# A four-layer decoder trunk in split float32: five buffers for raw weights instead of three

## The chip, the cores and the metric

The kernel runs on one core of a Trainium2 chip. The metric is the device time of one execution in microseconds: the median of three runs of the kernel before is 860.79 us (860.39, 860.79 and 860.89). Beside those runs, one execution was recorded by the hardware profiler; it took 859.14 us, and its span from the first to the last instruction is 857.4 us, so 1.74 us lie outside the span. Trace times below are microseconds from the start of the span.

## The reference

The input x is 256 tokens of 1024 float32 values. Four residual layers follow each other, and a final norm; the third kind of mixer stands between a gated DeltaNet layer and a second pooling layer:

```python
for i in range(DEPTH):                      # 4
    kind, j = i % N_MIXERS, i // N_MIXERS   # 0, 1, 2, 0
    h = rmsnorm(x, norm_g[i])
    if kind == 0:
        y = pool_mixer(h, pool_w_in[j], pool_w_grp[j], pool_scale[j], pool_w_out[j])
    elif kind == 1:
        y = gdn_mixer(h, gdn_w_in[j], gdn_conv[j], gdn_a_log[j], gdn_dt_bias[j],
                      gdn_norm_g[j], gdn_w_out[j])
    else:
        y = mla_mixer(h, positions, ...)
    x = x + y.astype(x.dtype)
return rmsnorm(x, final_g)
```

The gated DeltaNet mixer works on chunks of 64 tokens. The part of it on which the argument below turns is a triangular solve in each of 8 heads:

```python
L = jnp.where(strict, jnp.einsum('bhnid,bhnjd->bhnij', k_beta, k) * decay, 0.0)
A = jnp.eye(C, dtype=L.dtype) + L
sol = lax.linalg.triangular_solve(A, rhs, left_side=True, lower=True)
```

where k comes out of the input projection, a causal convolution over four tokens, SiLU and a normalization over 128 channels.

## The kernel before

Nearly all work is matrix products of the 256 tokens with weights, in float32 by splitting: a matrix is written as a high part that TensorE can take in one pass, and a low part, the rest. Three products (high by high, high by low, low by high) are added in PSUM.

**A unit of weights** is two k-slices of 128 rows by 512 columns, 512 KB (some are single slices or 256 KB). The function `weights` brings it in: SP's queue issues the DMA (L104, or L108 for other layouts) into a tile `raw` of the pool `rawp` (4 KB in each of the 128 partitions); ScalarE casts each slice to the high part `whi` (L117); VectorE, for some slices POOL, subtracts it from `raw` to get `wlo` (L119). `whi` and `wlo` are tiles of the pool `ring`, nine places of 128x512 for each name. A raw place is free again when the subtraction of its second slice is done; a place in the ring when TensorE's last product with it is done. TensorE then does 24 products of 128x256 (L127, L128, L129), or as many columns in pieces of 512 (L167).

**What sets the order.** The kernel is written once, stage after stage. A scheduler orders the instructions of each engine when the kernel is built; it knows how many places each pool has, and so which DMA can be issued when. On the chip each engine then runs its list in order, waiting on semaphores. Pools without a number of places (the residuals and large tiles `s4`, the scratch pools `wa`, `wb`, `wh`, the PSUM pools) are sized by the same build. The first six units of the program are single slices (k0 to k5 of the first projection) in scratch places, not in `rawp`.

**The start.** SP loads x in four DMAs (L256), two for each of the two token tiles, gains (L276) and the first weights. Each tile is normalized (L209 on ScalarE, L291 on POOL, L303 and L308) and transposed by TensorE (L323, eight transposes a tile); then come the products k0 to k7 of the first projection for that tile.

**The DeltaNet layer** projects by parts named g0 to g3 (gates), k0, k1 (keys), q0, q1 (queries) and v0 to v3 (values). After k1: convolution on ScalarE and VectorE (L633, L636), SiLU to `kqT` (L669), transposes on TensorE (L675), squares and sums for the norm (L678, L679), powers on POOL (L657), the scale (L705), the products kT by kT (L688), and the matrix `LT` (L692 on VectorE). Then the triangular solve, in this order:

- SP writes the diagonal blocks (32x32) of `LT` to DRAM, `d_l`, in eight DMAs, four for each token tile (L718), and reads them back in another layout, `Lb` (L721);
- POOL does 31 steps of forward substitution, a product `pr` (L726) and a subtraction into `Tb` (L730) each;
- SP writes `Tb` to DRAM, `d_t` (L732), and reads it back as `T` in eight DMAs (L736);
- TensorE puts the inverses of the blocks together, with copies by VectorE and ScalarE between: per token tile L806 (with T and LT), copy L808, L812, subtraction L815 (the stage "pairs"); then transposes L820, copy to T on ScalarE L821, products L824, copy to X on VectorE L827, products L830, subtraction L833 (the stage "whole").

Beside this TensorE projects what does not need the solve: queries, values and gates. The values' transposes are L778, their scaling on ScalarE is L781, and L847 multiplies them by the inverse. From L869 on the recurrence over chunks runs. The output projection uses the weights `gdn_w_out`.

Of the kernel before, what the change touches and what calls it, by code (L numbers as in the profile page):

```python
# [42 lines left out]
def trunk(ctx: ExitStack, tc: tile.TileContext, x, positions, norm_g, pool_w_in, pool_w_grp,  # L43
# [10 lines left out]
    E1 = 4  # L54
    const = ctx.enter_context(tc.tile_pool(name="const", bufs=1))
    s4 = ctx.enter_context(tc.tile_pool(name="s4"))
    rawp = ctx.enter_context(tc.tile_pool(name="rawp", bufs=3))
    ring = ctx.enter_context(tc.tile_pool(name="ring", bufs=9))
    wa = ctx.enter_context(tc.tile_pool(name="wa"))
    wb = ctx.enter_context(tc.tile_pool(name="wb"))  # L60
# [1169 lines left out]
def build(inputs, **opts):  # L1230
    import numpy as np
    import concourse.bacc as bacc

    nc = bacc.Bacc("TRN2", target_bir_lowering=False, num_devices=1)
    arrays, args = {}, []
    for name in _INS:
        a = np.ascontiguousarray(inputs[name])
        arrays[f"in_{name}_dram"] = a
        args.append(nc.dram_tensor(f"in_{name}_dram", a.shape, mybir.dt.from_np(a.dtype),
                                   kind="ExternalInput").ap())  # L1240
    args.append(nc.dram_tensor("out_0_dram", inputs["x"].shape, F32, kind="ExternalOutput").ap())
    with tile.TileContext(nc, schedule_with_timeline_sim=True, auto_bufs=True) as tc:
        trunk(tc, *args, **opts)
    return nc, arrays
# [8 lines left out]
```

## Time and profile before

| | |
|---|---|
| median of the runs | 860.79 us (860.39 to 860.89) |
| the profiled execution | 859.14 us |
| its span | 857.4 us |
| mean granted TensorE clock | 0.990 |
| read from HBM | 137.79 MB, 163 GB/s over the span |

The profile's page gives the busy time of each engine and groups of instructions (line, engine, operation, tiles written and read, count, busy time, mean time in ns, idle time ahead of it and what ended that). Engine names: PE is TensorE, PEld its weight loads, DVE VectorE, ACT ScalarE, SP the engine whose queue (SPq) issues nearly all DMAs. The trace answers further views: waits (who waited for which line, in total, how often, the longest), windows (busy time and granted TensorE clock in stretches of time), the timeline of one engine, and the chain of waits that ended last. In the windows, TensorE is busy this much of each 100 us:

```profile
0.00:100.00 100.00, 94.05 (x690) 89.46 (x691) 72.29 (x132) 60.38 (x110) 16.11 (x73) 0.98 0.64 202
100.00:200.00 100.00, 99.61 (x702) 91.75 (x701) 62.52 (x110) 56.53 (x105) 13.30 (x19) 1.00 0.59 185
200.00:300.00 100.00, 100.00 (x769) 95.72 (x768) 81.91 (x181) 64.18 (x124) 62.04 (x76) 1.00 0.56 169
300.00:400.00 100.00, 91.61 (x551) 80.22 (x550) 61.78 (x121) 50.71 (x126) 25.58 (x55) 0.95 0.33 100
400.00:500.00 100.00, 99.62 (x711) 93.22 (x710) 65.01 (x120) 59.65 (x128) 13.10 (x28) 1.00 0.61 177
500.00:600.00 100.00, 100.00 (x732) 93.76 (x731) 74.64 (x161) 56.55 (x131) 6.12 (x4) 1.00 0.58 154
600.00:700.00 100.00, 99.62 (x680) 90.29 (x679) 69.79 (x159) 58.48 (x144) 7.58 (x14) 1.00 0.47 143
700.00:800.00 100.00, 100.00 (x812) 98.37 (x811) 73.70 (x109) 58.08 (x98) 4.79 (x10) 1.00 0.61 194
```

The columns are: length; busy time (and instructions) of PE, PEld, DVE, ACT, POOL; granted clock; share of the DMA engines; GB/s. The first and the fourth row are those with idle time: the start, and the stretch around the triangular solve (the DeltaNet layer runs from about 200 to 400 us).

### The profile page before, as it was taken

Reading aid. Unit: us, or ns where it says so; the run is one execution under the profiler, and the core shown is the slowest. Engines: PE = TensorE matmul, PEld = TensorE weight load, DVE = VectorE, ACT = ScalarE, POOL = GpSimd, SP = SyncE. Lnnn points to the kernel's source line nnn. Section 1 sums busy time; section 2 is a strip of 40 time slices with the busy share of each in tenths; the row PEclk is TensorE's granted clock in tenths of the full one; section 3 lists DMA queues with packets and bytes.
Section 4 is the critical chain, followed back from the end, with each engine's and each line's share of the span. In section 5 each row is a group of like instructions: output and inputs, shape, how many; then the busy total and the mean of one; then the engine's idle time right before and its main releaser. Section 6 shows DMA issues by size and latency. Waiting matters only on the chain.

```text
span 857.4 us, 16137 instructions
## 1 busy us (share of the span) xinstructions
PE 835.0 (97%) x5967; PEld 778.7 (91%) x5967; DVE 591.2 (69%) x1138; ACT 488.2 (57%) x1007; POOL 155.7 (18%) x292
## 2 busy tenths in 40 slices
PE   7999999999999969999999999999999999999996
PEld 6999998988999959888979998999989989999986
DVE  4589776456989665656577659778767668866852
ACT  5565555467857435555565654566555476555542
POOL 4000000233248941022212002000000210000012
PEclk9999999999999989999999999999999999999999
DMA  6765556546555462222547676743652547565551
GB/s 199 249 188 188 178 189 213 180 148 206 188 160 176 134 168 102 75 74 99 173 147 215 201 165 172 196 132 95 171 167 79 173 149 218 175 192 183 187 200 50
DMA packets 111288, 140.43 MB, mean 164 GB/s; under 512 B 23340, under 2 KB 53224, under 8 KB 111208
## 3 DMA queue, kind: packets, MB, share of 16 engines
q1 hardware_dynamic: 109056, 138.17, 53.1%
q8 instruction: 47, 0.77, 0.4%
q0 software_dynamic: 320, 1.06, 0.3%
q10 hardware_dynamic: 1832, 0.16, 0.2%
q14 instruction: 33, 0.27, 0.1%
HBM read 137.79 MB, written 1.58 MB: 163 GB/s over the span
## 4 chain that ended last, share of the span: by engine, by line
PE 85%; POOL 7%; DVE 2%; DMA 2%; issue 2%; ACT 1%; SPq 1%; POOLq 0%; ACTq 0%; DVEq 0%
PE acc L167 34%; PE acc L127 12%; PE acc L128 12%; PE acc L129 12%; POOL Tb L730 2%; POOL pr L726 2%; PE aux L127 2%; PE aux L128 2%; PE aux L129 2%; DVE h L303 1%; DMA gain<-in_norm_g_dram 1%; PE aux L688 1%; ACT junk L209 1%; PE aux L806 1%; PE tp L1165 1%
## 5 line engine op out<-in xcount | busy, mean ns | idle before, releaser
L119 DVE TENSOR_TENSOR wlo<-raw,whi 128x512 fp32r<-128x512 f32 (+1 forms) x491 | 338.6, 712 | 163.2 <-ACT whi L117 160.9
L117 ACT CAST whi<-raw 128x512 fp32r<-128x512 f32 (+1 forms) x508 | 301.4, 617 | 261.8 <-PE acc L167 89.8
L127 PE MATMUL acc<-hTh,whi 128*128 128x256 f32 x832 | 235.3, 283 | 1.0 <-DVE cv L636 1.0
L128 PE MATMUL acc<-hTl,whi 128*128 128x256 f32 x832 | 235.8, 283 | 0.0
L129 PE MATMUL acc<-hTh,wlo 128*128 128x256 f32 x832 | 234.7, 282 | 0.0
L127 PEld LDWEIGHTS acc<-hTh,whi 128*128 128x128 f32 x832 | 157.7, 190 | 1.8 <-issue 1.4
L128 PEld LDWEIGHTS acc<-hTl,whi 128*128 128x128 f32 x832 | 157.6, 189 | 0.4
L129 PEld LDWEIGHTS acc<-hTh,wlo 128*128 128x128 f32 x832 | 157.5, 189 | 0.2
L167 PE MATMUL acc<-wlo,yTh 128*128 128x256 f32 (+1 forms) x384 | 116.2, 319 | 0.0
L167 PE MATMUL acc<-whi,yTh 128*128 128x256 f32 (+1 forms) x384 | 116.2, 323 | 0.0
L167 PE MATMUL acc<-whi,yTl 128*128 128x256 f32 (+1 forms) x384 | 92.4, 321 | 0.0
L167 PEld LDWEIGHTS acc<-wlo,yTh 128*128 128x128 f32 x384 | 72.0, 188 | 5.0
L167 PEld LDWEIGHTS acc<-whi,yTh 128*128 128x128 f32 x384 | 71.9, 188 | 5.2
L167 PEld LDWEIGHTS acc<-whi,yTl 128*128 128x128 f32 x384 | 63.1, 188 | 5.6
L291 POOL TENSOR_TENSOR hg<-x,gain 128x256 f32<-128x256 f32 x18 | 14.8, 832 | 259.1 <-DVE x L353 257.4
L167 PE MATMUL acc<-wlo,hTh 128*128 128x512 f32 (+1 forms) x144 | 55.9, 394 | 0.4 <-DVE wlo L119 0.2
L167 PE MATMUL acc<-whi,hTh 128*128 128x512 f32 (+1 forms) x144 | 55.5, 393 | 0.7 <-ACT hTh L195 0.7
L167 PE MATMUL acc<-whi,hTl 128*128 128x512 f32 (+1 forms) x144 | 45.4, 388 | 0.0
L119 POOL TENSOR_TENSOR wlo<-raw,whi 128x512 fp32r<-128x512 f32 x17 | 23.1, 1360 | 70.2 <-ACT whi L117 70.2
L434 POOL COPY win<-u 128x4 f32<-128x4 f32 x8 | 2.8, 354 | 177.0 <-ACT u L428 177.0
L167 PEld LDWEIGHTS acc<-wlo,hTh 128*128 128x128 f32 x144 | 27.3, 190 | 6.8 <-DVE wlo L119 1.7
L167 PEld LDWEIGHTS acc<-whi,hTh 128*128 128x128 f32 x144 | 27.3, 190 | 6.8 <-ACT hTh L195 1.7
(337 smaller groups left out, 1443.3 us busy)
## 6 DMA issues: line engine op xcount, KB each, us to landing
raw<-in_pool_w_in_dram SPq DMA_DIRECT2D x60, 512.0 KB, 4.4
raw<-in_gdn_w_in_dram SPq DMA_DIRECT2D x48, 512.0 KB, 3.9
raw<-in_pool_w_out_dram SPq DMA_DIRECT2D x32, 512.0 KB, 3.7
raw<-in_mla_w_in_dram SPq DMA_DIRECT2D x24, 512.0 KB, 4.4
raw<-in_mla_w_uq_dram SPq DMA_DIRECT2D x36, 256.0 KB, 3.8
raw<-in_pool_w_grp_dram SPq DMA_DIRECT2D x16, 512.0 KB, 4.2
raw<-in_gdn_w_out_dram SPq DMA_DIRECT2D x16, 512.0 KB, 3.5
raw<-in_mla_w_ukv_dram SPq DMA_DIRECT2D x32, 256.0 KB, 3.4
```

The source lines that it names most:

```text
L117: a = nc.scalar.copy(hi, v)
L119: b = e.tensor_tensor(out=lo, in0=v, in1=hi.bitcast(F32), op=ALU.subtract)
L127: nc.tensor.matmul(o, lhsT=lhs[0], rhs=rhs[0], start=start, stop=False)
L128: nc.tensor.matmul(o, lhsT=lhs[0], rhs=rhs[1], start=False, stop=False)
L129: nc.tensor.matmul(o, lhsT=lhs[1], rhs=rhs[0], start=False, stop=stop)
L167: nc.tensor.matmul(o, lhsT=act(k, t * P, P)[x], rhs=parts[j][z][:, sl], start=k == first and x == z == 0, stop=k == last and x == 1)
L209: nc.scalar.activation(junk[:, :n], src, AF.Square, scale=scale, accum_out=o)
L291: nc.gpsimd.tensor_tensor(out=self.early[t, a], in0=xs[t][:, sl], in1=self.g[:, sl], op=ALU.mult)
L303: nc.vector.scalar_tensor_tensor(out=h[:, cut:], in0=xs[t][:, sl], scalar=r[:, 0:1], in1=self.g[:, sl], op0=ALU.mult, op1=ALU.mult)
L688: nc.tensor.matmul(ps[:, b], lhsT=kT[hf][:, b, tt], rhs=rhs[hf][:, b, tt], start=True, stop=True)
L726: nc.gpsimd.tensor_tensor(out=pv, op=ALU.mult, in0=Lb[:, r, r + 1:, None].to_broadcast([M * Q, n, c]), in1=Tb[:, r:r + 1, :c].to_broadcast ...
L730: nc.gpsimd.tensor_tensor(out=tv, in0=tv, in1=pv, op=ALU.subtract)
```

## The change

One number: the pool `rawp` gets five places in place of three, 8 KB more in each partition. The ring keeps its nine.

```diff
     s4 = ctx.enter_context(tc.tile_pool(name="s4"))
-    rawp = ctx.enter_context(tc.tile_pool(name="rawp", bufs=3))
+    rawp = ctx.enter_context(tc.tile_pool(name="rawp", bufs=5))
     ring = ctx.enter_context(tc.tile_pool(name="ring", bufs=9))
```

Since the scheduler orders each engine's list by what it can start, the number moves instructions all over the program. Every engine does the same instructions as before; the lists differ. Three places matter below.

The list of SP's queue at the start (a piece of the difference; - is before, + is changed; `x_93` and `x_94` are the first and second token tile of x, two halves each):

```order
 L256 DMA x_93<-in_x_dram 128x512 x2
-L276 DMA gain<-in_norm_g_dram 128x512
 L104 DMA raw<-in_pool_w_in_dram 128x512
-L276 DMA gain<-in_norm_g_dram 128x512
+L276 DMA gain<-in_norm_g_dram 128x512 x2
 L104 DMA raw<-in_pool_w_in_dram 128x512 x3
-L256 DMA x_94<-in_x_dram 128x512 x2
-L104 DMA raw<-in_pool_w_in_dram 128x512 x2
+L256 DMA x_94<-in_x_dram 128x512
+L104 DMA raw<-in_pool_w_in_dram 128x512 x4
 L104 DMA raw<-in_pool_w_in_dram 128x2x512
-L104 DMA raw<-in_pool_w_in_dram 128x512 x2
+L256 DMA x_94<-in_x_dram 128x512
```

The second half of `x_94` goes from ahead of five weight DMAs to behind them. On TensorE, the transposes of the second token tile (L323) move from behind the products k0 to k3 of the first tile to behind its k0 to k7.

The list of SP's queue in the DeltaNet layer, around the triangular solve:

```order
-L104 DMA raw<-in_gdn_w_in_dram 128x2x512 x28
-L718 DMA d_l<-LT 32x8x32 x4
-L104 DMA raw<-in_gdn_w_in_dram 128x2x512
-L718 DMA d_l<-LT 32x8x32 x4
-L104 DMA raw<-in_gdn_w_in_dram 128x2x512
+L104 DMA raw<-in_gdn_w_in_dram 128x2x512 x33
+L718 DMA d_l<-LT 32x8x32 x8
+L104 DMA raw<-in_gdn_w_in_dram 128x2x512 x2
 L721 DMA Lb<-d_l 64x1024
-L104 DMA raw<-in_gdn_w_in_dram 128x2x512 x15
+L104 DMA raw<-in_gdn_w_in_dram 128x2x512 x13
+L104 DMA raw<-in_gdn_w_out_dram 128x2x512 x2
```

Ahead of the writes of LT stand 33 units where 28 stood, ahead of Lb 35 where 30 stood, and between Lb and the write of Tb (d_t, which follows) 15 as before.

TensorE's list in the last part of the inverse, from the second token tile's L824 to the first L869, before (`U`, `X`, `T` and `LT` are the inverse's tiles, `vc` a value after its convolution, `kqT` keys or queries, `vR` scaled values):

```order
L824 MATMUL aux<-T,LT 128x64 x8
L778 MATMUL tp<-ident,vc 128x128 x8
L830 MATMUL aux<-U,X 64x64 x8
L688 MATMUL aux<-kqT 128x128 x8
L847 MATMUL aux<-vR,U 128x256 x7
L869 MATMUL aux<-u_4252,ktok 128x256
```

Ahead of these six rows stand the first tile's L830 and the second's L820, and between that L820 and this L824 14 products L167 of a projection. The same part after the change, from the second tile's L812 on (`hTl_2268` is a piece of the layer's normalized input):

```order
L812 MATMUL aux<-U,X_3504 96x64 x8
L820 MATMUL aux<-ident,U 64x64 x8
L167 MATMUL acc<-whi,hTl_2268 128x512
L778 MATMUL tp<-ident,vc 128x128 x4
L824 MATMUL aux<-T,LT 128x64 x8
L675 MATMUL tp<-ident,kqT 128x128 x4
L830 MATMUL aux<-U,X 64x64 x8
L820 MATMUL aux<-ident,U 64x64 x8
L675 MATMUL tp<-ident,kqT 128x128 x4
L824 MATMUL aux<-T,LT 128x64 x8
L830 MATMUL aux<-U,X 64x64 x8
L688 MATMUL aux<-kqT 128x128 x8
```

The steps of the inverse stand closer together here, because the first L806 has moved to a later place: from the first L806 up to the first L869 TensorE's list has 115 rows before and 53 after the change (a row with x8 counted as one).

## The prediction

> **What bounds the kernel now.** I read the page first, then TensorE's waits, then everybody's waits, then the half-clock stretch by windows, and last the chain of waits through the one long gap of TensorE. The page's head and its first two groups:
>
> ```profile
> span 857.4 us, 16137 instructions
> PE 835.0 (97%) x5967; PEld 778.7 (91%) x5967; DVE 591.2 (69%) x1138; ACT 488.2 (57%) x1007; POOL 155.7 (18%) x292
> L119 DVE TENSOR_TENSOR wlo<-raw,whi 128x512 fp32r<-128x512 f32 (+1 forms) x491 | 338.6, 712 | 163.2 <-ACT whi L117 160.9
> L117 ACT CAST whi<-raw 128x512 fp32r<-128x512 f32 (+1 forms) x508 | 301.4, 617 | 261.8 <-PE acc L167 89.8
> ```
>
> TensorE is busy 835.0 of 857.4 us; all others have slack. What a place for raw weights can buy lies in the remaining 22.4 us. TensorE's waits say what fills them (us in total, times, longest):
>
> ```profile
> PE aux L806 <- DMA T<-d_t: 7.4, 1, 7.4
> PE tp L323 <- DVE h L303: 3.0, 2, 1.6
> PE tp L270 <- POOL ident masks.py:199: 2.0, 1, 2.0
> PE tp L323 <- ACT h L308: 1.0, 1, 1.0
> PE acc L127 <- DVE cv L636: 1.0, 1, 1.0
> PE acc L167 <- ACT hTh L195: 0.7, 3, 0.2
> PE acc L167 <- DVE wlo L119: 0.2, 1, 0.2
> ```
>
> For split weights TensorE waits 0.2 us in the whole program. The longest wait, 7.4 us, is for T, the result of POOL's substitution. The start (L270, L323) costs 6.0.
>
> Upstream there are waits, which is what the change addresses:
>
> ```profile
> SPq L104 <- DVE wlo L119: 464.3, 178, 23.6
> ACT whi L117 <- DMA raw<-in_gdn_w_in_dram: 29.5, 16, 6.2
> ACT whi L117 <- DMA raw<-in_pool_w_in_dram: 17.4, 13, 3.2
> ACT whi L117 <- PE acc L167: 89.8, 73, 2.7
> ACT whi L117 <- PE acc L128: 81.0, 106, 3.7
> ```
>
> SP's queue stands 464 us for a raw place, which the subtraction frees. ScalarE waits 29.5 and 17.4 us for raw data, but 89.8 and 81.0 for TensorE to free a place in the ring, whose nine places stay. So loading runs as far ahead as the ring lets it; two more raw places move the wait, and TensorE already waits for none of it. **The steady state I cost at nothing**, for the cover is TensorE's own work, 170 products of 128x256 in 20 us:
>
> ```profile
> 100.00:120.00 20.00, 20.00 (x171) 20.00 (x170) 12.18 (x19) 11.07 (x20) 0.23 (x1) 1.00 0.64 192
> ```
>
> That is 0.117 us a product, 2.8 for one unit of 512 KB (24 of them). The bound below is a loss of nothing; above, the 0.2 us that are there.
>
> **The gap at L806.** What the new order can change is the way from k1's last transposes to T. In the chain of waits (start, duration), SP's row of the four DMAs for the second half of LT standing between:
>
> ```profile
> 238.05 0.22 PE tp L675 x2
> ...
> 248.37 0.48 DVE LT L692 x2
> ...
> 251.18 0.39 SPq L104
> ...
> 253.11 2.87 DMA d_l<-LT
> 256.10 3.62 DMA Lb<-d_l
> ...
> 310.12 2.94 DMA d_t<-Tb
> 313.98 2.02 DMA T<-d_t
> 316.09 3.65 PE aux L806 x16
> ```
>
> From the transposes to L806 the chain takes 316.09 − 238.05 = 78.0 us; POOL's part, from Lb's landing at 259.7 to d_t at 310.1, is 50.4. TensorE stood ready at 316.09 − 7.36 = 308.73. The idleness costs twice, since the clock falls (time, busy time of the engines, clock, DMA):
>
> ```profile
> 306.00:309.00 3.00, 2.73 (x24) 2.53 (x22) 1.87 (x4) 1.14 (x2) 2.61 (x6) 1.00 0.70 224
> 309.00:316.00 7.00, 0.00 (x0) 0.00 (x0) 1.60 (x3) 1.81 (x4) 1.18 (x4) 0.85 0.56 134
> 316.00:324.00 8.00, 7.91 (x37) 7.94 (x38) 4.88 (x6) 2.83 (x7) 0.00 (x0) 0.50 0.71 214
> 324.00:326.00 2.00, 2.00 (x22) 2.00 (x20) 0.00 (x0) 2.00 (x7) 0.00 (x0) 0.96 0.03 8
> ```
>
> A clock of 0.85 over 7 us is 2.1 us at half speed, so it fell at 313.9; 0.96 over 2 us puts its return at 324.16. TensorE thus worked 8.07 us at half speed and lost 4.0. The gap is worth 7.4 + 4.0 = 11.4 us.
>
> **The change, part by part.**
>
> *1. Where L806 stands.* I count TensorE's rows in both orders, each by its duration in the trace. The last L675 stands behind 6.2 us more work than before, the first L806 behind 8.5 us more: three units later. If the chain keeps its 78.0 us, L675 is at 244.25, T at 322.3; TensorE arrives at 308.73 + 8.5 = 317.2 and waits 5.1 in place of 7.36: **−2.3 us**. Bounds of this term: nothing, if the chain grows by 2.3, and −7.4, if T is there first.
>
> *2. The chain itself.* SP issues 33 weight DMAs ahead of d_l in place of 28, then the eight d_l in one piece (the 0.39 of the row at 251.18 goes, and the 0.4 around it), then two more units and Lb. Those two need the places of units whose splits are done some 2 us before d_l can have landed, so SP should not hold Lb up, but 1 MB is in flight beside it, against 0.5 before. Gain 0.4 to 0.8, loss 0 to 1: I take **0**. Behind Lb, SP's queue holds 13 + 2 weights ahead of d_t in place of 15: no more. VectorE's and ScalarE's splits for the units brought forward stand ahead of LT's convolutions; the 6.2 us already count them as far as TensorE's rows moved with them. The bounds are −1 and +4 (five more units, at 0.7 us for each VectorE subtraction, if half stood in the way).
>
> *3. The half clock* returns if the wait does. It fell 5.2 us into the gap and stayed 10.24 (313.92 to 324.16). With a wait of 5.1 the loss is half of what is left of 10.24 when T comes, between 3.2 and 5.1, against 4.0: **+0.1**. How short must a gap be to escape? The start has a low stretch too, of 3.41 us, a third of 10.24; so I take time in cells of 3.41 and look at the cell ahead of it (TensorE's windows; the last row is the cell in which the gap of before begins):
>
> ```profile
> 6.72:10.13 3.41, 1.04 (x7) 1.00 0.98 359
> 10.13:13.54 3.41, 2.79 (x9) 0.50 1.03 390
> ...
> 307.09:310.51 3.42, 1.64 (x14) 1.00 0.39 141
> ```
>
> Busy 1.04 of 3.41 us was followed by half clock, so an idle piece of 2.4 in one cell is enough, and a gap of 5.1 always has that (at worst it is cut in two halves of 2.55). The Trainium skill (TensorE: Matmul & The Clock Gate, Part 1: The HAM clock gate) has a free-running window of 3413 ns and a throttle after at least one idle window; the 10.24 us are three such windows, which agrees, but the row at 6.72 speaks against a wholly idle one. By the page's words a gap of 5.1 would escape in (6.83 − 5.1)/3.41, half of the cases, and then the sum would be 4 us lower; that is a rival below, and I go by the row.
>
> *4. The way from T to L869* loses its cover. Before, weight products stand between most of the inverse's steps; now, by the order shown above, L812, L820, L824, L830, L820, L824, L830 and L688 follow each other with a few transposes between. Each step waits for a copy:
>
> ```profile
> 333.60 0.58 ACT L821 COPY T<-aux 64x512 f32<-64x512 f32 x1 [1.39 <-PE aux L820]
> 340.11 0.69 DVE L827 COPY X<-aux 64x512 f32<-64x512 f32 x1 [0.22 <-PE aux L824]
> 316.38 1.56 ACT L781 ACTIVATE vR<-tp,rki 128x256 f32<-128x256 f32 x4
> 328.48 0.60 PE L675 MATMUL tp<-ident,kqT 128*128 128x128 f32 x4
> ```
>
> Four transposes (0.60) cover nearly all of a copy (0.58 or 0.69, and 0.2 for the hand-over both ways): 0.2 to 0.3 are left at each of three places, all 0.9 at the last L830, behind which nothing stands. The values' transposes (L778) are now inside this stretch too, and their scaling on ScalarE, 1.56 us for four, must be done before L847 can use them: 0 to 4. I take 1 and have 0.8 + 0.9 + 1 = **+2.7**, bounds 0.9 and 6.
>
> *5. The start.* The second half of x's second token tile is issued behind five more weight DMAs:
>
> ```profile
> 5.34 1.39 SPq L256 DMA_DIRECT2D x<-in_x_dram  x2
> 16.49 1.10 PE L323 MATMUL tp<-ident,h 128*128 128x128 f32 x8 [1.01 <-ACT h L308]
> ```
>
> It lands some 2 us later, and its norm and transposes (L323, 16.49) with it. TensorE has k4 to k7 of the first tile to do meanwhile, 12 products of 0.23 = 2.8 us, and the wait of 1.0 in that row may go. From −1.0 (that wait gone) to +2.0 (no cover): **+0.5**.
>
> *6. The other layers* keep TensorE's order or change it by a few products, without waits of TensorE there before: 0, ±1.
>
> Sum: −2.3 + 0 + 0.1 + 2.7 + 0.5 + 0 = **+1.0 us**. The profiled execution took 859.14 (1.74 beyond the span), so 860.1; the median of the runs is 860.79, 1.65 higher, so **861.8**.
>
> **Rivals.**
>
> *Faster: T escapes the half clock.* POOL's steps are not of constant length; the same step took
>
> ```profile
> 273.04 0.89 POOL L726 TENSOR_TENSOR pr<-Lb,Tb 64x220 f32<-64x220 f32 x1
> 295.74 0.55 POOL L726 TENSOR_TENSOR pr<-Lb,Tb 64x220 f32<-64x220 f32 x1
> ```
>
> so it depends on what runs beside it, and other work does now. If the 50.4 us shrink by 2.7 or more (5%), the wait falls below 2.4 and the clock stays: −2.7 − 4.1 beside the sum, 861.8 − 6.8 = 855.0. Against it: the splits beside POOL are as many. Smaller gains, with part 4 at its lower bound, give 859.
>
> *Faster: the clock holds through the gap.* Low stretches came after cells that were 1.04 of 3.41 us busy and wholly idle; the cell at 307.09, with 1.64 of work, was followed by full clock. If the point lies close under that, or a gap cut into two halves isn't counted, 4.1 go: 857.7. The row at 6.72 speaks against it. (This is the result that the Trainium skill's page named above gives in half of the cases.)
>
> *Slower: LT comes later than TensorE's rows say.* L806 has a fixed place and nothing behind it may pass, so every us by which VectorE's earlier splits hold LT's convolutions back is a us lost. It ends slower from 0.7 us of delay on; with the +2 to +4 of part 2, or the 6 of part 4, it is 864 to 866. For it: SP, ScalarE and VectorE all run in order, and all have more weight work ahead of LT.
>
> *Slower by the start*: +2.0 in place of 0.5, 863.3.
>
> *Nothing happens*: the ring decides, gap and tail shift together, 860.8.
>
> **How the numbers follow.** Forecast 0.43 (860.0 to 863.5; a quarter of it beyond the bound). Faster 0.25 (T early enough to escape 0.08, the clock holding through the gap 0.07, smaller gains 0.10), slower by LT or the tail 0.17, by the start 0.07, nothing 0.08. About 0.2%, 1.7 us, can be told from no change. Within it: 0.32 + 0.08 = 0.40; slower 0.11 + 0.17 + 0.07 = 0.35; faster 0.25. The range leaves out a tenth on either side: 855.5 (most of the clock rival outside) to 866.0.
>
> **What would show it.** TensorE's wait at L806 for T of 4 to 6 us, T some 6 us later than 316.1; half clock for some 10 us behind it; new waits of TensorE of 0.2 to 1 us at L824, L830 and L847; waits for wlo still near nothing; ScalarE's waits for raw data smaller, for TensorE larger. I am wrong if T is late by more than 8 us or the half clock is missing, if TensorE waits at L323 by over 2 us more, or if a wait shows in the pool or attention layers.

## The result, and the profile after

The changed kernel takes 874.08 us (median of four runs, 872.84 to 874.62), the kernel before 860.59 in the same session (860.07 to 860.89): **1.0155 times as long** (95% interval 1.0138 to 1.0173), 13.5 us slower. The forecast was 861.8 with a range up to 866.0; it was wrong. The profiled execution took 874.11, its span is 872.3, 14.9 us over the span before.

The page's head after the change, with the busy time of each engine:

```profile
span 872.3 us, 16127 instructions
PE 841.8 (96%) x5967; PEld 782.1 (90%) x5967; DVE 593.8 (68%) x1138; ACT 490.4 (56%) x1007; POOL 155.4 (18%) x292
```

TensorE does the same 5967 products, is busy 6.8 us longer (a product at half clock takes longer and counts as busy for as long) and idle 8.1 us longer. Its waits after the change (us in total, times, longest):

```profile
PE acc L167 <- POOL wlo L119: 5.9, 2, 5.4
PE tp L323 <- DVE h L303: 4.1, 1, 4.1
PE acc L167 <- ACT hTh L195: 3.4, 5, 0.7
PE aux L806 <- DMA T<-d_t: 3.1, 1, 3.1
PE tp L270 <- POOL ident masks.py:199: 2.0, 1, 2.0
PE tp L675 <- ACT kqT L669: 1.2, 1, 1.2
PE acc L167 <- DVE wlo L119: 1.1, 3, 0.6
PE aux L830 <- DVE X L827: 1.0, 2, 0.8
```

L806 waits 3.1 us for T in place of 7.4. That looks like a gain, but the first row is new: just ahead of L806 a product waits 5.4 us for a low part that POOL makes. The start costs more (4.8 for L323 in place of 4.0), L675 waits where it did not, and L830 waits as foreseen.

Upstream the two places do what they are for. ScalarE's waits for loaded weights are nearly gone (29.5 and 17.4 us before), and those for TensorE to free the ring have grown (89.8 and 81.0 before):

```profile
ACT whi L117 <- PE acc L167: 122.4, 81, 8.5
ACT whi L117 <- PE acc L128: 112.3, 149, 2.7
...
ACT whi L117 <- DMA raw<-in_pool_w_in_dram: 4.7, 2, 2.8
```

**Where the 14.9 us come from.** Both kernels have the same products, so the two traces can be laid beside each other by work done: TensorE's products are added up in the order of each trace, each at its full-clock duration, and the times at which equal sums are reached are compared. (Where the order differs, the products at that sum differ, but not the amount of work.)

| TensorE's work done, us at full clock | where | reached before | reached after | after − before |
|---|---|---|---|---|
| 13 to 160 | after the first projection's start, to the end of the first layer | 21.3 … 169.4 | 24.3 … 172.4 | +3.0 |
| 175 | first products of the DeltaNet layer | 185.6 | 190.3 | +4.7 |
| 220 | after k1's transposes L675 | 231.3 | 238.3 | +7.0 |
| 240 | projections beside the solve | 251.8 | 258.5 | +6.7 |
| 310 | behind the gap at L806 | 335.7 | 343.3 | +7.5 |
| 342 | recurrence runs | 368.7 | 383.3 | +14.5 |
| 812 | end | 849.9 | 864.8 | +14.9 |

So the start costs 3.0, the way past k1's last L675 another 3.7, the gap itself with its half clock 0.8, and the stretch from the inverse into the recurrence 7.0. These are the numbers of one profiled execution of each kernel. The attention layer and the last layer, some 470 us of work, cost 0.4 together.

*The solve's chain.* SP's queue around it, after (start, duration, number of issues):

```profile
263.25 4.51 SPq L718 DMA_DIRECT2D d_l<-LT  x8
267.86 0.91 SPq L104 DMA_DIRECT2D raw<-in_gdn_w_in_dram  x2
269.03 0.54 SPq L721 DMA_DIRECT2D Lb<-d_l  x1
...
327.67 0.47 SPq L732 DMA_DIRECT2D d_t<-Tb  x1
```

and POOL's timeline in the solve, with what ended the idle time before a step in brackets:

```profile
276.92 0.23 POOL L726 TENSOR_TENSOR pr<-Lb,Tb 64x31 f32<-64x31 f32 x1 [6.88 <-DMA Lb<-d_l]
...
305.70 1.25 POOL L119 TENSOR_TENSOR wlo<-raw,whi 128x512 fp32r<-128x512 f32 x1
306.92 0.67 POOL L730 TENSOR_TENSOR Tb<-Tb,pr 64x252 f32<-64x252 f32 x1
```

Lb is issued at 269.03 against 256.10: 12.9 us later, which are the 6.2 us of work that the prediction counted ahead of the last L675 and the 6.7 by which TensorE was late by then. Then Lb is in flight for 276.92 − 269.03 = 7.9 us, against 3.6 of the row in the prediction: two units, 1 MB, are issued just ahead of it. POOL's part takes 327.67 − 276.92 = 50.7 against 50.4. Together 12.9 + 4.3 + 0.3 = 17.5, and T is read at 333.50 instead of 316.09, 17.4 later. POOL also has splits in its list (L119), and the one at 305.70 stands behind a solve step and ahead of another (306.92), though its high part had been ready since 294.8; TensorE waits for it.

TensorE's timeline at the two waits and in the last part of the inverse:

```profile
307.01 0.80 PE L167 MATMUL acc<-wlo,hTh 128*128 128x512 f32 x1 [5.45 <-POOL wlo L119]
...
333.50 3.65 PE L806 MATMUL aux<-T,LT 128*128 128x64 f32 x16 [3.08 <-DMA T<-d_t]
...
356.59 1.14 PE L830 MATMUL aux<-U,X 64*64 64x64 f32 x16 [0.20 <-DVE X L827]
...
358.97 2.98 PE L824 MATMUL aux<-T,LT 64*128 64x64 f32 x16
362.74 1.97 PE L830 MATMUL aux<-U,X 64*64 64x64 f32 x16 [0.79 <-DVE X L827]
364.63 3.78 PE L688 MATMUL aux<-kqT 128*128 128x128 f32 x16
```

The second L830 takes 1.97 us where the first took 1.14: the clock fell in between. The half clock now comes four times inside the kernel, where it came twice before. TensorE's windows, in the cells of 3.41 us that the steps of the granted clock mark (time, length, busy time and products, clock, DMA):

```profile
301.72:305.13 3.41, 0.00 (x0) 1.00 0.00 0
329.03:332.44 3.41, 1.40 (x6) 1.00 0.82 226
356.34:359.75 3.41, 3.13 (x36) 1.00 0.11 40
359.75:363.16 3.41, 2.62 (x15) 0.50 0.00 0
363.16:366.57 3.41, 3.41 (x24) 0.50 0.00 0
366.57:369.98 3.41, 3.41 (x14) 0.50 0.00 0
```

One stretch is that of the start, now two cells long (8.18 to 15.00). The first two rows are cells ahead of low stretches of 6.8 us each (from 305.13 and from 332.44): idle and more than half idle, as the prediction had it. The third is not: 3.13 us busy, by the profile's modelled ends of products, with short products of 64 rows, and then three cells at half clock.

### The profile page after: what moved, and what is told of

It is laid out like the page before. It is cut to its first block, busy times and chain, and to the rows that moved or that the text cites. A ratio compares the mean times of both kernels' runs of the same rounds, so it can differ in the third digit from the quotient of the medians.

```text
span 872.3 us, 16127 instructions
## 1 busy us (share of the span) xinstructions
PE 841.8 (96%) x5967; PEld 782.1 (90%) x5967; DVE 593.8 (68%) x1138; ACT 490.4 (56%) x1007; POOL 155.4 (18%) x292
## 4 chain that ended last, share of the span: by engine, by line
PE 85%; POOL 6%; ACT 2%; DMA 2%; issue 2%; DVE 1%; SPq 0%; ACTq 0%; POOLq 0%; DVEq 0%
PE acc L167 33%; PE acc L127 12%; PE acc L128 12%; PE acc L129 12%; PE aux L127 2%; POOL Tb L730 2%; POOL pr L726 2%; PE aux L128 2%; PE aux L129 2%; PE aux L688 1%; DMA gain<-in_norm_g_dram 1%; PE tp L323 1%; ACT whi L117 1%; DMA Gb<-d_g 1%; PE aux L806 1%
## 5 line engine op out<-in xcount | busy, mean ns | idle before, releaser
L119 DVE TENSOR_TENSOR wlo<-raw,whi 128x512 fp32r<-128x512 f32 (+1 forms) x491 | 340.0, 716 | 154.6 <-ACT whi L117 153.1
L167 PE MATMUL acc<-wlo,yTh 128*128 128x256 f32 (+1 forms) x384 | 115.2, 318 | 0.0
L167 PE MATMUL acc<-whi,yTh 128*128 128x256 f32 (+1 forms) x384 | 113.8, 322 | 0.0
L167 PE MATMUL acc<-whi,yTl 128*128 128x256 f32 (+1 forms) x384 | 91.9, 321 | 0.0
L167 PEld LDWEIGHTS acc<-wlo,yTh 128*128 128x128 f32 x384 | 71.7, 188 | 5.4
L167 PEld LDWEIGHTS acc<-whi,yTh 128*128 128x128 f32 x384 | 70.8, 188 | 5.7 <-ACT yTh L197 0.3
L167 PEld LDWEIGHTS acc<-whi,yTl 128*128 128x128 f32 x384 | 62.5, 188 | 5.0
L167 PE MATMUL acc<-wlo,hTh 128*128 128x512 f32 (+1 forms) x144 | 57.9, 408 | 7.0 <-POOL wlo L119 5.9
L167 PE MATMUL acc<-whi,hTh 128*128 128x512 f32 (+1 forms) x144 | 56.7, 403 | 3.4 <-ACT hTh L195 3.4
L167 PE MATMUL acc<-whi,hTl 128*128 128x512 f32 (+1 forms) x144 | 47.7, 403 | 0.0
L167 PEld LDWEIGHTS acc<-wlo,hTh 128*128 128x128 f32 x144 | 28.2, 196 | 15.4 <-POOL wlo L119 6.6
L167 PEld LDWEIGHTS acc<-whi,hTh 128*128 128x128 f32 x144 | 28.0, 195 | 9.9 <-ACT hTh L195 4.7
L167 PEld LDWEIGHTS acc<-whi,hTl 128*128 128x128 f32 x144 | 27.2, 196 | 4.8
```

Of the source, the lines that this page charges most:

```text
L119: b = e.tensor_tensor(out=lo, in0=v, in1=hi.bitcast(F32), op=ALU.subtract)
L167: nc.tensor.matmul(o, lhsT=act(k, t * P, P)[x], rhs=parts[j][z][:, sl], start=k == first and x == z == 0, stop=k == last and x == 1)
```

## The experiments

Two theories at the start. **Theory 1:** the lists cost the time, that is the order into which the scheduler puts each engine's work when it has five places; the places themselves cost nothing. **Theory 2:** the places cost it, since weights run further ahead on the chip and their traffic stands in the way of the solve's small DMAs.

To part them, the lists of one kernel are given to the other. In the kernels called pinned, a table ORDER names each engine's instructions in the order of the kernel that is copied, and edges that only bind the order of issue (nothing waits for them on the chip) make the scheduler keep it (`kind` is such an edge, `by` the instructions by name). In the traces of the four kernels that are pinned as a whole, each engine's list is that of the kernel copied, but for one instruction of ScalarE in three of them that stands a place earlier or later:

```diff
+    for text in ORDER.values():
+        names = []
+        for part in text.split():
+            a, _, n = part.partition("+")
+            names += [f"I-{int(a) + k}" for k in range(int(n or 0) + 1)]
+        names = [n for n in names if n in by]
+        for p, q in zip(names, names[1:]):
+            tc.add_manual_dep(by[q], p, kind, reason="order")
```

**Three places with the new lists** (the number of places of before, every engine's list from the changed kernel):

> Three places, but every engine issues its instructions in the order of the changed kernel (issue-order edges from each listed instruction to the next). Theory 1 (the loss lies in the lists alone): 874 us, within 2. Theory 2 (the loss comes from the places, more transfers in flight at once slow the small DMAs of x, LT and T): 861 to 865. If the lists need the places (SP then waits for a place ahead of the writes of LT): above 876.

Measured: 879.52 us (878.44 to 880.16), ratio 1.0234 (1.0214 to 1.0254). The new lists cost more than the whole change, without the new places.

**Four places with the old lists** (five places with them were not tried):

```diff
-    rawp = ctx.enter_context(tc.tile_pool(name="rawp", bufs=3))
+    rawp = ctx.enter_context(tc.tile_pool(name="rawp", bufs=4))
```

> Four places, every engine in the order of the kernel before. Theory 1 (lists alone): 860.6, within 1.7, SP's waits for a place shorter. Theory 2 (more in flight): 862 to 867, the wait for T above 7.4 us.

Measured: 865.83 (864.12 to 867.00), ratio 1.0071 (1.0049 to 1.0093). Taken alone this speaks for theory 2. But pinning may have a price of its own, so two controls were run.

**Three places with the old lists**, which is the kernel before but for the edges:

> Control for pinning: three places and the lists of the kernel before, as edges. Same instructions in the same order as the kernel before; only places in PSUM differ, and these are the same as in the run with four places and the old lists (865.8). If that run was slow for its fourth place: 860.6 here. If it was slow for the places in PSUM that pinning gives: 865 to 866 here.

Measured: 863.77 (863.15 to 864.12), ratio 1.0054 (1.0039 to 1.0069). Pinning costs some 4.6 us by itself. Lists and raw places are the same; what differs is which bank of PSUM a product gets, since the pinned build hands them out in another order. That the banks make the price was not tested: new waits of up to 0.6 us show in its recurrence, and part of the price was not placed.

**Five places with the new lists**, the changed kernel but for the edges:

> Control for pinning: five places and the lists of the changed kernel, as edges; places in PSUM as in the run with three places and the new lists (879.5). If that run was slower than the changed kernel for want of two places: 874 here. If for its places in PSUM: 879 here. So with the three other pinned runs: lists old or new by places three or more, all else equal.

Measured: 875.46 (873.00 to 878.36), ratio 1.0181 (1.0156 to 1.0206). The four pinned kernels together:

| | old lists | new lists |
|---|---|---|
| three places | 1.0054 | 1.0234 |
| four (old) or five (new) | 1.0071 | 1.0181 |

With three places the new lists cost 1.8% (1.0234 / 1.0054 = 1.0179); with the five places that they were made for they cost 1.3% over the old lists (1.0181 / 1.0054 = 1.0126). A place more costs the old lists nothing that can be told (the intervals overlap), and two places more give the new lists 0.5% back. Pinning itself costs the new lists 0.3% (1.0181 against 1.0155, the intervals overlap) and the old ones 0.5%, both less than the order. Theory 2 falls, as far as the fourth place goes for the old lists: the order costs the time, and the places, taken alone, help a little where the order asks for them.

**The start alone.** Three places, pinned only up to the first projection's units: SP's list and the others' from the changed kernel there, and free behind.

> Three places; only the instructions traced up to the first projection's units (loads of x, norms, first weights, their splits and products) are in the changed kernel's order among themselves, the rest is ordered by the scheduler. If the start's loss is due to the second token tile's half behind five weight DMAs, and is carried through: 860.6 + 3.0 = 863.6, with TensorE's wait at L323 of 4 us. If a delay at the start is absorbed later (the chain to T has its own slack): 861.

Measured: 863.31 (862.62 to 865.27), ratio 1.0050 (1.0033 to 1.0067), 4.3 us. TensorE's waits in it:

```profile
PE tp L323 <- DVE h L303: 2.6, 1, 2.6
...
PE tp L323 <- ACT h L308: 1.5, 1, 1.5
```

Hardly any of the loss at the start is made up for later: by work done the profiled execution is 4.4 late behind the start and 4.0 at the end. A low stretch of 3.4 us (23.09 to 26.51) that the changed kernel does not have adds to it. The reverse, **five places with the old start:**

> Five places; the start alone in the order of the kernel before, the rest ordered by the scheduler. By the start's share: 874.1 - 3.0 = 871.1. If the later losses come from the start's delay: below 868. If the start does not count: 874.

Measured: 871.79 (869.14 to 874.23), ratio 1.0141 (1.0113 to 1.0169), less than the change's 1.0155 by 1.2 us, though the intervals overlap. The start is a part of the loss, and not the largest.

**POOL's two splits earlier.** Pinned to the new lists, except that POOL's splits at 305.70 and 308.23 go to an earlier place in the solve (a and b are the tiles `raw` that they read; steps are named by the shape of their product):

```diff
 L730 Tb<-Tb,pr 64x240
+L119 wlo<-raw a
 L726 pr<-Lb,Tb 64x247
 L730 Tb<-Tb,pr 64x247
 L726 pr<-Lb,Tb 64x252
 L730 Tb<-Tb,pr 64x252
+L119 wlo<-raw b
...
 L726 pr<-Lb,Tb 64x252
-L119 wlo<-raw a
 L730 Tb<-Tb,pr 64x252
 L726 pr<-Lb,Tb 64x247
-L119 wlo<-raw b
 L730 Tb<-Tb,pr 64x247
```

> As the run with five places and the new lists, but two of POOL's weight subtractions in the substitution stand earlier in POOL's list (seven and five steps of the substitution). TensorE's wait of 5.4 us for POOL's wlo goes. If that wait is a loss of its own: 5.4 and half of its 6.8 us of half clock, some 8 us, faster than the run with the new lists. If it stands in the shadow of T (the substitution ends when it ends): TensorE comes to L806 earlier and waits there 8 to 11 us in place of 3, total within 2 us of that run.

Measured: 877.50 (874.75 to 878.98), ratio 1.0210 (1.0187 to 1.0234), no faster than the 1.0181 of its base. TensorE's wait for POOL is gone, and its first wait now reads

```profile
PE aux L806 <- DMA T<-d_t: 10.8, 1, 10.8
```

in place of 3.7. The wait for POOL stood in the shadow of the later wait for T: taking it away moves the time, 7.1 us, into the next wait. T is read when it was read before (332.71 against 332.96). The test is not clean: at the earlier place POOL waits 1.8 us for ScalarE's high part and its solve takes 52.1 us in place of 50.6, while Lb happens to come 1.0 sooner.

**The last part of the inverse filled.** Pinned to the new lists, with products that nobody reads (six transposes of the identity each) ahead of the second L824 and of both L830, as cover for the copies and to keep the clock:

```diff
-                ps = bank(aux, "aux").rearrange("p (m c) -> p m c", m=H)
+                ps = bank(aux, "aux")
+                for _ in range(6 if t else 0):
+                    nc.tensor.transpose(ps[:, :P], ident, ident)
+                ps = ps.rearrange("p (m c) -> p m c", m=H)
...
-                ps = bank(aux, "aux").rearrange("p (m c) -> p m c", m=H)
+                ps = bank(aux, "aux")
+                for _ in range(6):
+                    nc.tensor.transpose(ps[:, :P], ident, ident)
+                ps = ps.rearrange("p (m c) -> p m c", m=H)
```

> As the run with five places and the new lists, with 18 idle transposes of the identity by TensorE added in the inverse's last steps: six ahead of L830 of the first token tile, six ahead of L824 and six ahead of L830 of the second. They add 2 to 3.8 us of work, of which 1 lies in the waits there. If the clock fell at 360 us because of what TensorE did in the 3.4 us ahead (short 64-row products, little idle time): full clock after it, 10.2 us of half clock gone, total 1 to 3 us faster. If it falls anyway: 2 to 4 us slower.

Measured: 874.37 (873.00 to 874.62), ratio 1.0175 (1.0159 to 1.0190), the same as its base within the intervals. The clock is repaired. TensorE's window of the base:

```profile
358.00:371.00 13.00, 12.21 (x63) 0.50 0.00 0
```

and of the filled kernel:

```profile
358.00:371.00 13.00, 11.70 (x88) 1.00 0.01 1
```

Half of 12.21 busy us at half clock is 6.1. Of that, 18 dummy products, at the 0.116 us that one takes in the run with 24 of them below, use up 2.1, and TensorE, now earlier, waits 0.9 for ScalarE's scaled values (L781), a row that the base does not have. The profiled spans differ by 4.2 (876.7 and 872.5), the medians by 1.1; the base's profiled execution is the longest of its four runs. So the gain lies between nothing and 4, and the medians don't show it to be one.

**Lb ahead of the two units.** Pinned to the new lists; only SP's list differs:

```diff
+L721 DMA Lb<-d_l 64x1024
 L104 DMA raw<-in_gdn_w_in_dram 128x2x512 x2
-L721 DMA Lb<-d_l 64x1024
```

> As the run with five places and the new lists (875.5), but the read of Lb stands on SP's queue ahead of the two weight DMAs that stood before it. In the changed kernel Lb landed 7.9 us after its issue, with 1 MB issued just ahead of it; in the kernel before 3.6. If the weights ahead make it late: Lb lands 3.5 to 5 us earlier, T with it, POOL's subtractions too, so TensorE's waits of 5.4 and 3.7 us shrink by 4 to 5 us together and the total by 4 to 6. If Lb is late for another cause (the write of LT behind it): no change, 875.

Measured: 872.75 (870.19 to 875.64), ratio 1.0148 (1.0120 to 1.0177), 2.7 us below its base (less than expected, and the intervals overlap). SP's queue in it, and behind it POOL's first step:

```profile
268.69 0.53 SPq L721 DMA_DIRECT2D Lb<-d_l  x1
```

```profile
272.39 0.23 POOL L726 TENSOR_TENSOR pr<-Lb,Tb 64x31 f32<-64x31 f32 x1 [2.79 <-DMA Lb<-d_l]
```

3.7 us from issue to use in place of 7.9. The two units were the cause of the longer flight. Tb was written out 3.6 us earlier (L732 at 323.52 against 327.15).

**All four repairs together** (old start, Lb ahead, POOL's splits earlier, the filled inverse):

> Five places, new lists with all four repairs: the start in the old order (3.0), Lb ahead of two weights (4), POOL's two subtractions earlier, 18 idle transposes in the inverse's last steps (4). If these are the places where the loss is, and they add: 875.5 - 11 = 864.5, within 2, about what three places and the old lists take when pinned (863.8). If a loss only moves on to the next wait: 868 or more.

Measured: 872.38 (871.49 to 873.83), ratio 1.0146 (1.0127 to 1.0165), eight us above what was expected. With Lb earlier, POOL reaches the place of the moved split before ScalarE has made the high part:

```profile
291.25 1.29 POOL L119 TENSOR_TENSOR wlo<-raw,whi 128x512 fp32r<-128x512 f32 x1 [4.44 <-ACT whi L117]
```

POOL stands 4.4 us in the middle of the solve, which takes 323.70 − 268.55 = 55.2 us instead of 50.7, and L806 waits 10.7. An edit that neither gained nor lost clearly when it was alone takes back what another gains.

**Without POOL's edit, three repairs** (old start, Lb ahead, the filled inverse):

> As the run with four repairs, but POOL's two subtractions where the new lists have them (five places, new lists, old start, Lb ahead of two weights, 18 idle transposes in the inverse's last steps). If the fourth repair took the others back (POOL waited 4.4 us for ScalarE there, and T with it): d_t 4 to 5 us earlier, half clock at L806 short or absent, 864 to 867. If the losses do not add: 870 to 873 as with four.

Measured: 870.10 (869.11 to 871.07), ratio 1.0117 (1.0101 to 1.0132), 2.3 us below four repairs. That is at the lower end of what was expected if the losses do not add, and 3 us above the range for POOL's edit as the whole cause: the solve is back at 50.9 us and L806 waits 6.7, but 10.2 us at half clock still go with that wait. Against the base 5.5 us of the loss are gone, and 6.5 us of span remain over the pinned kernel with the old lists (868.5 − 862.0). By work done, against the pinned kernel with the old lists: 1.2 at the start, 1.7 in the DeltaNet layer's first products, 1.7 at L675, −2.3 over the gap, and 4.2 from the filled inverse on, of which the dummies are 2.1. The waits ahead of L675 were not tried: it stays open which moved instruction of ScalarE or VectorE makes them.

**Four places, lists free.** Is the loss a matter of how many places there are?

> Four places, lists by the scheduler, nothing pinned. If the loss grows with the weights that run ahead of LT: between 860.6 and 874, 866 to 870. If it is the accident of one order: anywhere from 858 to 876; T's lateness at L806 then tells.

Measured: 882.57 (879.04 to 883.20), ratio 1.0253 (1.0232 to 1.0275), worse than five and above both expectations. TensorE's waits:

```profile
PE acc L167 <- POOL wlo L119: 6.5, 2, 6.0
PE aux L806 <- DMA T<-d_t: 4.9, 1, 4.9
...
PE tp L675 <- ACT kqT L669: 2.4, 1, 2.4
```

The losses stand where they stand with five places, and 20.5 us at half clock follow the gap at L806 (334.22 to 354.70). From three over four to five places the time goes 860, 883, 874: it does not rise with the number. That the order which falls out of it decides is the reading of the pinned runs; the lists of this kernel were not pinned.

**The gap of the kernel before, filled.** Three places, lists free; 24 dummy transposes ahead of the first L806 and one edge that keeps them behind the last product ahead of it:

```diff
+                for _ in range(24 if t == 0 else 0):
+                    nc.tensor.transpose(ps[:, :P], ident, ident)
```

> The kernel before with 24 idle transposes of the identity by TensorE in the gap ahead of L806, issued behind the last product there; the rest is ordered by the scheduler, as before but for a few rows. The half clock behind the gap cost 4.0 us. If idleness alone brings it: full clock behind L806, total 860.6 - 4.0 = 856.6. If the transposes push T back or the clock falls anyway: 860 to 862.

Measured: 861.17 (859.44 to 862.22, 11 runs), ratio 1.0015 (1.0005 to 1.0025): no gain. The 24 dummies took 2.78 us (0.116 each) and left 4.6 us of wait; the clock fell all the same, 2.8 us later and for 6.8 us in place of 10.2, and once more for 3.4 us at 354.2. TensorE's windows:

```profile
309.00:316.00 7.00, 3.05 (x28) 1.00 0.58 152
316.00:324.00 8.00, 7.36 (x37) 0.57 0.74 216
```

**The same with 60 dummies**, which fill the gap to its end:

> The kernel before with 60 idle transposes in the gap ahead of L806 (0.108 us each by the run with 24: 6.5 of the 7.4 us). If idleness brings the half clock: none at 314 to 324, 4 us less than the kernel before, 856 to 857. If something else in the gap does: as with 24, 860 to 861.

Measured: 857.55 (856.24 to 860.36, 11 runs), ratio **0.9975** (0.9963 to 0.9987): 0.25% faster than the kernel before, and the fastest kernel of the study. L806 (L809 here) waits 0.7, and the clock stays, by the same view. In this run and the last the scheduler also moved a few rows of TensorE, VectorE and ScalarE, but on TensorE and VectorE the same ones in both, so the 36 dummies more are what parts them:

```profile
308.00:316.00 8.00, 7.35 (x68) 1.00 0.58 155
316.00:324.00 8.00, 7.40 (x68) 1.00 0.71 214
```

## Why the prediction was wrong

**Right.** The steady state cost nothing: over 147 us of work in the first layer the distance of the two kernels keeps within 0.1 us, and over 470 behind the inverse it ends 0.4 larger; the wait for raw weights moved to the ring as foreseen. The counts of moved work held: 6.2 us more ahead of the last L675 show up in Lb's issue (12.9 = 6.2 + 6.7). The half clock returned with the gap (part 3). The prediction's first sign of being wrong, T late by more than 8 us, came: T is 17.4 late, where it had some 6. L830 waits 1.0 us for the copies, as part 4 had it with 0.9 at the last one.

**Part 5, the start: right place, size off.** The term was +0.5, from bounds of −1.0 and +2.0; it measured +3.0 by work done (alone, 4.3 by the ratio of the runs). The step that failed is "it lands some 2 us later, and its norm and transposes (L323, 16.49) with it". Five weight DMAs do not pass SP's queue in 2 us. SP's queue after the change:

```profile
5.12 0.85 SPq L256 DMA_DIRECT2D x<-in_x_dram  x1
6.01 4.50 SPq L104 DMA_DIRECT2D raw<-in_pool_w_in_dram  x5
10.82 0.34 SPq L256 DMA_DIRECT2D x<-in_x_dram  x1
```

The last quarter of x is issued at 10.82, some 5 us later, and the second tile's transposes come at 21.66 instead of 16.49. The products k4 to k7 of the first tile cover 2.8 of these 5.2 us, as counted; 2.4 are lost by then, and the first product behind waits another 0.7 for hTh. The first token tile is late as well, which part 5 did not look at. Its first transposes, before and after:

```profile
8.44 0.66 PE L323 MATMUL tp<-ident,h 128*128 128x128 f32 x4 [1.34 <-DVE h L303]
10.21 1.11 PE L323 MATMUL tp<-ident,h 128*128 128x128 f32 x4 [4.07 <-DVE h L303]
```

VectorE makes this h and waits for the gains until 8.88 in place of 7.63; in SP's list a weight now stands ahead of them. What each of the two delays would cost alone was not tried. By work done, the seven profiled executions with the new order at the start are 2.2 to 4.4 us late behind it against the kernel before, the other seven with the old order −0.4 to 1.2. The second cell at half clock is not the order's doing: of the kernels pinned with three places, the one with the old lists has two cells, the one with the new lists one.

**Part 6 and the stretch ahead of the last L675: +3.7, not in the sum.** "The other layers keep TensorE's order or change it by a few products" was costed at nothing within 1. The DeltaNet layer's own first products and its L675 were not looked at: 1.7 us go at the layer's start, where TensorE waits 0.7 for hTh and 1.0 for two low parts (0.2 each before), and 2.0 around L675 (1.2 for kqT and 0.7 for keys scaled by VectorE). The forecast took the way to the last L675 as 6.2 us of TensorE's work and no wait.

**Part 2, the chain: 0 was wrong by 4.3.** The prediction saw that two units stood ahead of Lb, 1 MB in flight beside it, and gave that 0 to 1. It measured 4.3: the flight was 7.9 us, and 3.7 with the units moved behind.

**Part 1, L806 three units later: −2.3 was lost.** With the chain 4.3 longer, the wait would have been 5.1 + 4.3 + 0.3 = 9.7; the run with POOL's splits moved shows 10.8. That it reads 3.1 comes from the new wait for POOL just ahead of it, and that wait costs its own half clock. Gap and clock together: +0.8 in place of −2.3 + 0.1.

**Part 4, the way to L869: 7.0 in place of 2.7, the largest miss.** L830 waits 1.0 in all; the wait of L847 for the values, taken as 1, did not come. What was missed is a fourth low stretch, 359.75 to 369.98, in which TensorE worked 9.4 us at half speed: 4.7 lost. The remaining 1.3 were not placed. The prediction asked for the half clock only behind long gaps; here it followed a cell that was 3.13 us busy. The stretch is no accident of this execution, but its length differs: all five other profiled kernels with TensorE's new order here and nothing filled have one at this place (3.4 us in one, 10.2 to 13.7 in four), the three with the filled inverse have none, and of the six with the old order, or nearly so, one has 3.4.

Of the rivals, "slower: LT comes later than TensorE's rows say" was nearest, with 864 to 866. LT did come later, by the 2.0 us around L675; the chain's 4.3 have another cause than VectorE's splits, which that rival names, and the 7.0 lie beyond its bound of 6. The sum of the parts: predicted −2.2 for the gap, 2.7, 0.5 and 0; measured 0.8, 7.0, 3.0, and 3.7 + 0.4 that had no term.

## What to carry to other kernels

Where a scheduler orders the work, a number of buffers is an edit of every list: the buffers were harmless here as far as they were tried and the order cost 1.3 to 1.8%, so ask of such a change what it moves in front of the few short instructions that the critical chain needs, and pin the old order to see which of the two acts. A wait that hides in the shadow of a later one is worth nothing until the later one goes, and repairs of a chain have to be timed against each other. A gap that must stay could be kept at full clock here with dummy products that filled it to its end; dummies that left 4.6 us of it open gained nothing.

## What the runs showed that was not expected

- Low stretches of the granted clock, whole multiples of 3.41 us long, come also where TensorE is hardly idle: after a cell with 3.13 of 3.41 us busy, filled with products of 64 rows, came 10.2 us at half clock. Eighteen full-width dummy transposes among them took the stretch away in all three kernels that have them. Whether the size of the products or the pieces of idle time between them decide was not separated. The Trainium skill (TensorE: Matmul & The Clock Gate, Part 1: The HAM clock gate) has the clock fall after at least one idle window of 3413 ns; the length agrees with the cells here, the idleness does not (3.13 of 3.41 us busy). The Trainium skill's section on a second failure mode (the same page, A second HAM failure mode: psum-queue depth-cycling), where short idle pieces between groups of matmuls make the clock go back and forth, is nearer to this row.
- From the issue of Lb, a read of 256 KB, to POOL's first use of it passed 3.6 to 4.3 us with at most one unit issued shortly ahead (the kernel before and nine runs), and 6.9 to 7.9 with two units, 1 MB, just ahead of it (the changed kernel and four runs; 5.0 in a fifth, where SP issued Lb a microsecond later).
- The kernel before, pinned to its own lists, with the same places and other PSUM banks, took 0.5% longer (1.0039 to 1.0069); the cause was not placed.
